# Expert weights in 2 MB chunks with 16 KB rows, and slots chosen by their release

## The chip, the cores and the metric

The kernel runs on one core of a Trainium2 chip. The metric is the time of one execution on the device in microseconds (us), as the median of several runs. The profile shows one execution on the same core.

## The reference

The kernel computes one block of a streaming encoder for 256 tokens of 1024 channels in float32:

```python
ada = c_act @ w_ada + b_ada                      # six vectors of 1024, from the conditioning vector
h = rms_norm(x, norm_mix_g) * (1 + sc_m) + sh_m
x = x + g_m * hybrid_mixer(h)                    # latent attention and a gated convolution, w_in, w_o, ...
h = rms_norm(x, norm_ffn_g) * (1 + sc_f) + sh_f
logits = h @ router_w + router_b                 # 32 experts
top_val, top_idx = top_k(logits, 4); gate_w = softmax(top_val)
# for each expert e, for the tokens that chose it:
gu = h[tok] @ w_gu[e] + b_gu[e]                  # 1024 x 2048
act = (clip(up, -7, 7) + 1) * (g * sigmoid(1.702 * g)),  g = min(gate, 7)
y = act @ w_down[e] + b_down[e]                  # 1024 x 1024
x = x + g_f * sum over the four experts of gate_w * y
return rms_norm(x, norm_final_g)
```

The experts' weights are 32 x (8 MB + 4 MB) = 384 MB; everything else that is loaded is about 52 MB.

## The kernel before

The program has two stages. The front (to about 253 us) computes the conditioning vectors, the mixer and the router. Weights of the front come in 26 units of up to 1 MB (w_in, w_uq, w_ukv, w_up_conv, w_up_attn, w_o); `split` (line 333) turns each raw unit into a high part (ACT, line 336) and a low part (DVE, line 338), and three matmuls (lines 323 to 325, or 448) multiply with them. Between the units stand 16 chunks of w_ada (`ada_next`, line 420). The expert stage goes through 32 experts, each with a capacity of 64 tokens. `gather` (line 958) picks the tokens of four experts by a matmul with one-hot columns; `gate_up` (line 992) makes 64 matmuls with eight 1 MB chunks of w_gu (one chunk: 128 rows of 8 KB, one on each partition); `act` (line 1005) and `act_t` (line 1015, four transposes) follow; `down` (line 1030) makes 16 matmuls with four chunks of w_down (two rows of 4 KB on each partition); `scatter` (line 1044) adds two experts at a time to the result. `down` of an expert runs after `gate_up` of the next one. The last expert's w_down is loaded in columns (line 176, rows of 1 KB), so that the final norm can start on half of them. `beyond` (line 1061) is a branch for experts with more than 64 tokens, in the middle of the experts.

All weights and many intermediate tensors share one ring of 22 slots of 8 KB for each partition (`slot`, line 73): a new tile takes the place of the one that was made 22 tiles earlier, and what is written into it waits until that one was last read. x itself (`xs`) holds a slot too.

The order of work on each engine is the order of the program text (`manual_schedule`). All weight loads are issued by SP. SP goes through its own instructions alone: a load waits there until its slot is free, and all loads behind it wait as well; of the other engines' progress SP sees only what its slots wait for. In the front the order of the loads is written by hand (`queue`, line 361), with tables `LOOK` and `RAW` of how many units ahead are split and loaded. `prefetch(10)` at line 769 puts ten chunks of w_gu ahead of the last w_o units' splits in the text; `bias_load` (line 808, called at 899) loads the experts' bias into a slot of its own, with four loads on SP; `bias_table` (line 816) turns it into a table on ACT and POOL. All further loads of experts stand behind it.

Of the kernel before, what the change touches and what calls it, by code (L numbers as in the profile page):

```python
# [16 lines left out]
P = 128  # L17
D = 1024
# [21 lines left out]
NSLOT = 22  # L40
# [16 lines left out]
def block_kernel(ctx, tc, x, c, positions, w_ada, b_ada, norm_mix_g, w_in, q_norm_g, w_uq, kv_norm_g,  # L57
# [11 lines left out]
    slots = ctx.enter_context(tc.tile_pool(name="slots", bufs=NSLOT))  # L69
# [3 lines left out]
    def slot(shape, name="wslot", dtype=F32):  # L73
        t = slots.tile([P, 2048], dtype, name=name, tag="wslot")
        n = 1
        for s in shape:
            n *= s
        t = t[:, :n]
        if len(shape) == 2:
            t = t.rearrange("p (a b) -> p a b", b=shape[1])  # L80
        elif len(shape) == 3:
            t = t.rearrange("p (a b c) -> p a b c", b=shape[1], c=shape[2])
        return t
# [13 lines left out]
    xs = slot([NT, D], "xs")  # L97
# [10 lines left out]
    iota2 = keep.tile([P, 2, CAP], F32, name="iota2")  # L108
    G.iota(iota2, pattern=[[0, 2], [1, CAP]], base=1, channel_multiplier=0,
# [52 lines left out]
    todo = []  # L162
    for e in range(NE):
        todo += [(e, k) for k in range(NQ)]
        if e and e != NE // 2:
            todo += [(e - 1, k) for k in range(NQ, 12)]
        if e == NE // 2 - 1 or e == NE - 1:
            todo += [(e, k) for k in range(NQ, 12)]
    here = []

    def prefetch(n):
        while len(here) < n and todo:
            e, k = todo.pop(0)
            if e == NE - 1 and k >= NQ:

                w = slot([4, 2, 256])
                b = 4 * ((k - NQ) % 2)
                cols = ap_of(w_down, (e * DE + b * P) * D + 256 * ((k - NQ) // 2),
                             [[D, P], [P * D, 4], [512, 2], [1, 256]])
                for q in ([slice(0, 4)] if k % 2 == 0 else (slice(0, 2), slice(2, 4))):  # L180
                    for h in range(2):
                        load(w[:, q, h], cols[:, q, h])
            elif k < NQ:
                w = slot([2048])
                load(w, gu_v[:, e, k, :])
            else:
                w = slot([2, D])
                load(w, dn_v[:, e, k - NQ])
            here.append(w)

    with tc.tile_pool(name="front", bufs=1) as fr, \
# [13 lines left out]
        pos_i = ft("pos_i", [NT, P], 2, "pe0", I32)  # L205
# [14 lines left out]
        def rows_in(dst, src):  # L220
# [4 lines left out]
                 rows_in(pvec[8:16], norm_ffn_g.rearrange("o (q p) -> (o q) p", p=P)),  # L225
# [24 lines left out]
        def ada0_mm(j):  # L250
            ada_mm(pa, j, ada0[j])

        ss = keep.tile([P, NT], F32, name="ss")
        junk = ft("junk", [P, D], 1, "CT")
# [4 lines left out]
        xn = slot([NT, D], "xn")  # L259
# [31 lines left out]
        for q2 in range(4):  # L291
            p = (mmt() if q2 == 3 else tpt()).rearrange("p (q t) -> p q t", t=T)
            xps.append(p)
            for q in range(2):
                for i in range(NT):
                    TE.transpose(p[:, q, i * P:(i + 1) * P],
                                 xn[:, i, (2 * q2 + q) * P:(2 * q2 + q + 1) * P], ident)
        for j in range(6, 8):
            ada0_mm(j)
        ppc = mmt()  # L300
        TE.transpose(ppc[:, :48], pvec, ident[:48, :48])
        V.tensor_copy(pcol, ppc[:, :48])
        gmix, gffn, qg, kvg = pcol[:, 0:8], pcol[:, 8:16], pcol[:, 16:18], pcol[:, 18:19]
        cw = pcol[:, 19:31].rearrange("p (k q) -> p k q", q=4)

        def halves_t(row, pc):

            for q in range(4):
                TE.transpose(pc[:, q * P:(q + 1) * P], row[:, q * P:(q + 1) * P], ident)
            return pc.rearrange("p (q b r) -> p b q r", b=4, r=32)  # L310
# [4 lines left out]
        arow = ft("arow", [P, 512], 1, "CT")  # L315
        V.tensor_add(arow, brow[0], pa)
        pcv = halves_t(arow, mmt())
# [9 lines left out]
        def cut(pair, *idx):  # L327
            return [t[idx] for t in pair]


        lo_on = "VVVVVVVVVVVVVVVVVVVVVVVVVV"

        def split(raw, shape):
            hi = slot(shape, "whi", F32R)
            lo = slot(shape, "wlo", F32R)
            S.activation(hi, raw, AF.Copy)  # L336
            eng = V if lo_on[len(done)] == "V" else G
            eng.tensor_tensor(lo, raw, hi, op=ALU.subtract)  # L338
            return [hi, lo]
# [18 lines left out]
        raws, done, taken = [], [], [0]  # L358


        queue = list("wwwwwwwawwwwaaaawaawawwawwaaaawwwwwawwwaaw")

        def ada_fetch():
            g, j = ada_todo.pop(0)
            w = slot([2048])
            load(w, ap_of(w_ada, g * 2048 + j * 6 * D, [[8 * 6 * D, P], [1, 2048]]))
            ada_raw.append((g, j, w))

        def fetch(n):
            while len(raws) < min(n, len(jobs)):  # L370
                if queue.pop(0) == "a":
                    ada_fetch()
                else:
                    shape, src = jobs[len(raws)]
                    w = slot(shape)
                    load(w, src)
                    raws.append((w, shape))
# [8 lines left out]
        RAW = [0, 0, 2, 3, 2, 2, 3, 3, 2, 1, 0, 3, 4, 3, 1, 2, 5, 4, 5, 3, 1, 5, 4, 6, 6, 6]  # L386

        def unit():
            k = taken[0]
            taken[0] += 1  # L390
            fetch(k + 1 + LOOK[k] + RAW[k])
            ahead(k + 1 + LOOK[k])
            u = done[k]
            done[k] = None
            return u
# [4 lines left out]
        hT = [slot([NQ, T], "hTh", F32R), slot([NQ, T], "hTl", F32R)]  # L400
        h32 = slot([NQ, T], "h32")
# [11 lines left out]
        S.dma_start(rw, router_w.rearrange("o (q p) e -> p (o q) e", p=P))  # L413
# [3 lines left out]
        ada_todo = [(g, j) for g in (1, 2) for j in range(8)]  # L417
        ada_raw, ada_ps = [], {}

        def ada_next(n=1):  # L420
            for _ in range(n):
                g, j, w = ada_raw.pop(0)
# [21 lines left out]
        def proj(u, ps, half, n):  # L444
            for l, r in ((0, 0), (1, 0), (0, 1)):
                for i in range(NT):
                    for q in range(4):
                        TE.matmul(ps[i][:, :n], hT[l][:, 4 * half + q, i * P:(i + 1) * P], u[r][:, q, :],  # L448
                                  start=(half == 0 and q == 0 and l == 0 and r == 0),
                                  stop=(half == 1 and q == 3 and r == 1), skip_group_check=True)  # L450


        def projT(u, ps, half):
            for m in range(4):
                for q in range(4):
                    mul3(ps[m // 2][:, m % 2, :], cut(u, slice(None), q, slice(m * P, (m + 1) * P)),
                         cut(hT, slice(None), 4 * half + q), half == 0 and q == 0 and m % 2 == 0,
                         half == 1 and q == 3)

# [12 lines left out]
        qq = slot([NT, H, DQK], "qq")  # L472
        kk = slot([NT, H, DQK], "kk")
        vv = slot([NT, H, DV], "vv")
        lat = slot([NT, 384], "lat")
# [19 lines left out]
        CT = ft("CT", [P, 4, T])  # L495
# [53 lines left out]
        cuT = ft("cuT", [P, 4, T + 2])  # L549
        G.memset(cuT[:, :, 0:2], 0.0)  # L550
        for m2 in range(2):
            V.tensor_mul(cuT[:, 2 * m2:2 * m2 + 2, 2:], CT[:, 2 * m2:2 * m2 + 2, :], pu[m2])
# [5 lines left out]
        def qkt(hp):  # L558
            if hp % 2 == 0:
                qkT.append(slot([2, 4, T], "qkT"))  # L560
# [72 lines left out]

        zt = ft("zt", [P, 4, T], tag="CT")

        def conv():
            for m in range(4):
                S.activation(zt[:, m, :], cuT[:, m, 2:], AF.Copy, scale=cw[:, 2, m:m + 1])
            for m in range(4):
                for k in (1, 0):  # L640
                    V.scalar_tensor_tensor(zt[:, m, :], cuT[:, m, k:k + T], cw[:, k, m:m + 1], zt[:, m, :],
                                           op0=ALU.mult, op1=ALU.add)
# [6 lines left out]
        def halves(src, name, engs):  # L649

            t = slot([2, 4, T], name, F32R)
# [4 lines left out]
            return [t[:, 0], t[:, 1]]  # L656
# [3 lines left out]
        def gate(k):  # L660
# [3 lines left out]
            if k % 4 == 0:  # L664
                sg[k // 4] = slot([NT, D], "sg")
# [6 lines left out]
        def branch(src, us, out):  # L672
            ps = [mmt() for _ in range(4)]
            for k in range(2):
                for n in range(4):
# [5 lines left out]
                    if k:  # L681
                        out(i, hs, ps[n])
                yield
# [16 lines left out]
        qkt(3)  # L700
        gate(4)
# [5 lines left out]
        attn = ft("attn", [P, 4, T], tag="cuT")  # L707
# [5 lines left out]
        zT = halves(zt, "zT", (G, V))  # L713
# [3 lines left out]
        pr = scores(3)  # L717
        gate(7)
# [17 lines left out]
        V.tensor_copy(by_half(sh_col[:, 1, :]), halves_t(brow[1], tpt())[:, 2:4, :, 0])  # L736
# [5 lines left out]
        for k in range(4):  # L742
            gate(k)
            if k == 3:
                attnT = halves(attn, "attnT", (G, G))
# [4 lines left out]
        while ada_todo:  # L750
            ada_fetch()
# [11 lines left out]
        while ada_raw:  # L763
            ada_next()
        V.tensor_copy(by_half(a_col[:, 1, :]), halves_t(brow[2], tpt())[:, 0:2, :, 0])
# [13 lines left out]
        def wo_mm(i, h, q0, q1):  # L779
            if q0 == 0:  # L780
                wps[i][h] = mmt()
            for q in range(q0, q1):
                mul3(wps[i][h], cut(mT, slice(None), q, slice(i * P, (i + 1) * P)),
                     cut(wo[q // 2], slice(None), q % 2, slice(h * 512, (h + 1) * 512)), q == 0, q == NQ - 1)

# [8 lines left out]
        def x1_t(i, h):  # L794

            p = tpt().rearrange("p (q t) -> p q t", t=P)
            for q in range(4):
                TE.transpose(p[:, q, :], xs[:, i, (4 * h + q) * P:(4 * h + q + 1) * P], ident)
# [17 lines left out]
        def bias_table():  # L816
# [4 lines left out]
            G.tensor_tensor(bg2[64:], raw[64:], bg2[64:], op=ALU.subtract)  # L821
            for k in range(2):
# [44 lines left out]
        oh0 = ft("oh0", [P, NT, CAP], 1, "cuT")  # L867
# [411 lines left out]
```

## Time and profile before

| | |
|---|---|
| median of 3 runs | 1193.88 us (1189.0 to 1195.42) |
| the profiled execution | 1194.52 us, span 1192.8 us |
| PE busy | 1086.2 us, 91% |
| DVE, ACT, POOL busy | 341.5, 152.6, 29.4 us |
| moved by DMA | 457.70 MB, mean 384 GB/s over the span |
| first load of w_gu | issued at 178.90 us |
| first gate/up matmul | 254.02 us |

The profiled time and the span differ by what lies around the program. A busy PE is not PE at its peak, since matmuls are pipelined and their ends are modelled. The page cuts the span in 40 slices of 29.8 us; the chain of waits is followed back from the last instruction. A DMA in the chain lasts from its issue to its landing, so it includes the transfers ahead of it in the queue. SPq is SP's sequencer, which issues the loads.

### The profile page before, as it was taken

The page shows a single profiled execution, that of the slowest core. Times are in us where ns is not written, and L with a number is a line of the kernel's source. Part 1 is how long each engine was busy: PE and PEld are TensorE (multiplying, and loading weights), DVE is VectorE, ACT ScalarE, POOL GpSimd, SP SyncE. Part 2 cuts the span into 40 slices and gives each one's busy share as a digit, 9 for nine tenths or more (in the row PEclk, how much of TensorE's full clock was granted, in tenths as well). Part 3 has the DMA queues.
Part 4 walks back from the last instruction along what each step waited for, and adds up shares of the span by engine and source line. Part 5 has one row for each costly group of instructions (what it writes and reads, how often), then busy time and mean ns, then how long its engine had stood idle before and what let it go on. Part 6 is the DMA issues. An engine that isn't in the chain of part 4 may idle for free.

```text
span 1192.8 us, 12301 instructions
## 1 busy us (share of the span) xinstructions
PE 1086.2 (91%) x4968; PEld 483.8 (41%) x4968; DVE 341.5 (29%) x694; ACT 152.6 (13%) x261; POOL 29.4 (2%) x86
## 2 busy tenths in 40 slices
PE   5898998989999999999998879999888988898886
PEld 1887666754343343333332243343223322342223
DVE  3857544333221231122212121222112211222113
ACT  1545532212000010000000000010000000000001
POOL 1000001010000000000000000000000000000000
PEclk9898998979999999998999989999999999999999
DMA  9983778589999999999999999999999999999995
GB/s 363 339 330 149 275 309 352 196 347 397 417 417 417 417 416 417 417 417 417 417 417 417 414 419 416 416 417 416 418 417 416 417 417 417 418 417 418 417 415 204
DMA packets 91961, 457.70 MB, mean 384 GB/s; under 512 B 8495, under 2 KB 13648, under 8 KB 56060
## 3 DMA queue, kind: packets, MB, share of 16 engines
q1 hardware_dynamic: 90634, 456.59, 94.6%
q8 instruction: 41, 0.67, 0.2%
q10 hardware_dynamic: 1186, 0.14, 0.1%
q0 software_dynamic: 80, 0.14, 0.0%
q14 instruction: 20, 0.16, 0.0%
HBM read 455.79 MB, written 1.05 MB: 383 GB/s over the span
## 4 chain that ended last, share of the span: by engine, by line
PE 54%; DMA 41%; DVE 2%; ACT 1%; issue 1%; SPq 0%; DVEq 0%; ACTq 0%
DMA wslot<-in_w_gu 22%; PE pg L1001 18%; DMA wslot<-in_w_down 17%; PE pm L1027 10%; PE mm L448 5%; PE pm L969 4%; PE mm L1047 3%; PE mm L323 2%; PE mm L325 2%; PE mm L324 2%; DMA wslot<-in_w_ada 2%; PE pa L247 1%; PE pm L1018 1%; PE pg L1126 1%; DMA wslot<-in_w_in 1%
## 5 line engine op out<-in xcount | busy, mean ns | idle before, releaser
L1001 PE MATMUL pg<-wslot,hsel 128*64 128x512 f32 x2048 | 464.9, 602 | 32.6 <-DMA wslot<-in_w_gu 32.6
L1001 PEld LDWEIGHTS pg<-wslot,hsel 128*64 128x64 f32 x2048 | 139.3, 138 | 342.2 <-issue 245.4
L1027 PE MATMUL pm<-wslot,aT 128*64 128x512 f32 (+1 forms) x1056 | 231.9, 584 | 16.7 <-DMA wslot<-in_w_down 15.1
L1008 DVE TENSOR_SCALAR ga<-pg 128x512 f32<-128x512 f32 x32 | 22.1, 692 | 462.5 <-PE pg L1001 447.2
L1027 PEld LDWEIGHTS pm<-wslot,aT 128*64 128x64 f32 x1056 | 72.3, 137 | 171.7 <-issue 126.1
L1009 ACT ACTIVATE sgm<-ga 128x512 f32<-128x512 f32 x32 | 20.1, 630 | 695.7 <-DVE ga L1008 695.7
L1041 DVE TENSOR_TENSOR yp<-gfx,pm 64x512 f32<-64x512 f32 x62 | 42.5, 685 | 208.3 <-PE pm L1027 207.7
L338 DVE TENSOR_TENSOR wlo<-wslot,whi 128x2048 fp32r<-128x2048 f32 (+3 forms) x26 | 56.2, 2199 | 22.5 <-ACT whi L336 19.8
L969 PE MATMUL pm<-oh,xs 128*128 128x256 f32 (+1 forms) x256 | 58.2, 387 | 4.7 <-DVE oh L955 4.7
L969 PEld LDWEIGHTS pm<-oh,xs 128*128 128x128 f32 x256 | 48.9, 197 | 17.4 <-issue 11.2
L1047 PE MATMUL mm<-yp,s 128*128 128x512 f32 x120 | 54.9, 600 | 0.8 <-DVE yp L1041 0.8
L336 ACT ACTIVATE whi<-wslot 128x2048 fp32r<-128x2048 f32 (+3 forms) x26 | 46.8, 1840 | 17.3 <-DMA wslot<-in_w_in 12.5
L247 PE MATMUL pa<-wslot,cact 128*32 128x512 f32 x192 | 30.2, 718 | 12.3 <-DVE rs_v L116 8.5
L1047 PEld LDWEIGHTS mm<-yp,s 128*128 128x128 f32 x120 | 22.1, 190 | 30.0 <-issue 27.5
L1123 POOL CAST sel<-id 128x256 fp32r<-128x256 f32 x32 | 12.9, 403 | 816.4 <-PE pg L1126 816.4
L1018 PE MATMUL pm<-ident,sgm 128*128 128x128 f32 x128 | 20.9, 286 | 10.4 <-ACT s L989 7.9
L323 PE MATMUL mm<-hTh,whi 128*128 128x256 f32 x96 | 27.5, 287 | 0.0
L325 PE MATMUL mm<-hTh,wlo 128*128 128x256 f32 x96 | 27.2, 283 | 0.0
L324 PE MATMUL mm<-hTl,whi 128*128 128x256 f32 x96 | 27.2, 283 | 0.0
L448 PE MATMUL mm<-whi,hTh 128*128 128x512 f32 (+1 forms) x80 | 23.7, 440 | 3.0 <-ACT hTh L405 3.0
L1126 PE MATMUL pg<-bg,sel 128*128 128x512 f32 x64 | 24.2, 460 | 1.3 <-DVE hsel L156 1.3
L1020 DVE COPY aT<-pm 128x512 f32<-128x512 f32 x32 | 22.1, 691 | 8.3 <-PE pm L1018 6.6
(301 smaller groups left out, 755.2 us busy)
## 6 DMA issues: line engine op xcount, KB each, us to landing
wslot<-in_w_gu SPq DMA_DIRECT2D x256, 1024.0 KB, 20.1
wslot<-in_w_down SPq DMA_DIRECT2D x124, 1024.0 KB, 20.1
wslot<-in_w_ada SPq DMA_DIRECT2D x24, 1024.0 KB, 6.6
wslot<-in_w_in SPq DMA_DIRECT2D x14, 1024.0 KB, 6.5
wslot<-in_w_o SPq DMA_DIRECT2D x4, 1024.0 KB, 8.5
wslot<-in_w_up_conv SPq DMA_DIRECT2D x2, 1024.0 KB
wslot<-in_w_up_attn SPq DMA_DIRECT2D x2, 1024.0 KB, 4.9
wslot<-in_w_down SPq DMA_DIRECT2D x4, 512.0 KB, 8.4
```

Source lines behind the costliest of these rows:

```text
L247: TE.matmul(pa[32 * b:32 * b + 32, :], cact[:, j:j + 1].to_broadcast([P, 32]), w[:, b * 512:(b + 1) * 512], start=(j == 0), stop=(j == 7), ...
L323: TE.matmul(o, l[0], r[0], start=start, stop=False, skip_group_check=True)
L324: TE.matmul(o, l[0], r[1], start=False, stop=False, skip_group_check=True)
L325: TE.matmul(o, l[1], r[0], start=False, stop=stop, skip_group_check=True)
L336: S.activation(hi, raw, AF.Copy)
L338: eng.tensor_tensor(lo, raw, hi, op=ALU.subtract)
L448: TE.matmul(ps[i][:, :n], hT[l][:, 4 * half + q, i * P:(i + 1) * P], u[r][:, q, :], start=(half == 0 and q == 0 and l == 0 and r == 0), st ...
L969: TE.matmul(p[:, q, :], xs[:, i, qs], oh[:, i, :n], start=(i == 0), stop=(i == NT - 1))
L1001: TE.matmul(pg[64 * g:64 * g + 64, n, :], hs[k // 4][:, k % 4, c0:c0 + CAP], w[:, f0:f0 + 512], start=False, stop=(k == NQ - 1), skip_grou ...
L1027: TE.matmul(py[64 * h:64 * h + 64, :], aT[:, qa, 64 * g:64 * g + 64], w[:, h], start=(b == 0), stop=(b == 7), skip_group_check=True)
L1041: V.tensor_mul(yp[64 * k2:64 * k2 + 64, h * 512:(h + 1) * 512], gfx[hp, :], py[hp, :])
L1047: TE.matmul(acc[i][h], s2[:n, i * P:(i + 1) * P], yp[:n, h * 512:(h + 1) * 512], start=start, stop=False, skip_group_check=True)
```

## The change

The ring becomes a list of 22 slots (`Slots`). A tile takes the free slot that was given back longest ago in the order of the program text; once no load is left in the list, one whose neighbour is held comes first, so that neighbours come free together. Tiles are given back by hand (`give`, `drop`). Loads stand in one list (`loads`), and `pump` issues them after each `give` as long as more than `spare` slots are free; `need` issues what is due. x moves out of the slots; the convolution's, the latents' and the attention's tensors move into them.

After the front the 22 slots are joined in pairs to 11 slots of 16 KB (`wide`). Expert weights come in chunks of 2 MB: of w_gu two neighbouring rows (16 KB) lie on a partition, of w_down four neighbouring rows (16 KB). So channel 2(128a + p) + b is on partition p, and the tokens, the norm's columns and the transposes are read with a step of 2 (`fcols`) or 4 (`a[:, q::4]`). `prefetch(10)` is gone; the list of expert loads is filled behind the front's text.

```diff
-NSLOT = 22
+WIDE = 11
-    def slot(shape, name="wslot", dtype=F32):
-        t = slots.tile([P, 2048], dtype, name=name, tag="wslot")
+    class Slots:
+        def __init__(self, pool, since, size):
+            self.pool, self.since, self.held, self.clock, self.spare = pool, since, {}, max(since), 0
+            for i in range(len(since)):
+                pool.tile([P, size], F32, name="w", tag=f"w{i}", bufs=1)
+        def take(self, shape, dtype=F32):
+            i = min((not loads and self.since[(i ^ 1) % len(self.since)] is not None, c, i)
+                    for i, c in enumerate(self.since) if c is not None)[2]
+            self.since[i] = None
+            t = self.pool.tile([P] + list(shape), dtype, name="w", tag=f"w{i}", bufs=1)
+            self.held[id(t)] = (t, i)
+            return t
+        def give(self, *ts):
+            for t in ts:
+                self.clock += 1
+                self.since[self.held.pop(id(t))[1]] = self.clock
+            self.pump()
+        def pump(self):
+            while loads and sum(c is not None for c in self.since) > self.spare:
+                loads.pop(0)()
+    loads = []
+    def need(ready):
+        while not ready():
+            loads.pop(0)()
+    early = ctx.enter_context(ExitStack())
+    narrow = Slots(early.enter_context(tc.tile_pool(name="narrow", bufs=1)), [0] * (2 * WIDE), 2048)
+    slot, give, pump = narrow.take, narrow.give, narrow.pump
...
-    xs = slot([NT, D], "xs")
+    xs = keep.tile([P, NT, D], F32, name="xs")
...
-    gu_v = w_gu.rearrange("o e (q p) f -> p (o e) q f", p=P)
-    dn_v = w_down.rearrange("o e (k q p) d -> p (o e) k q d", q=2, p=P)
+    gu_v = w_gu.rearrange("o e (a p b) f -> p (o e) a b f", p=P, b=2)
+    dn_v = w_down.rearrange("o e (g p q) d -> p (o e) g q d", p=P, q=4)
+    def fcols(k):
+        return slice(256 * (k // 2) + k % 2, 256 * (k // 2) + 256, 2)
...
-                 rows_in(pvec[8:16], norm_ffn_g.rearrange("o (q p) -> (o q) p", p=P)),
+                 rows_in(gvec, norm_ffn_g.rearrange("o (a c) -> (o a) c", c=256)),
...
+        for b in range(2):
+            TE.transpose(ppc[:, 48 + 4 * b:52 + 4 * b], gvec[:, b::2], ident[:4, :4])
...
-        queue = list("wwwwwwwawwwwaaaawaawawwawwaaaawwwwwawwwaaw")
+        loads += [(chunks if c == "a" else units).pop(0) for c in "wwwwwwwwwaaawwawwwwaaaawwwaawaawwwawawaaww"]
+        narrow.spare = 9
         def ahead(n):
-            fetch(n)
             while len(done) < min(n, len(jobs)):
+                need(lambda: len(raws) > len(done))
                 done.append(split(*raws[len(done)]))
...
-        prefetch(10)
         wo = [unit(), unit()]
         next(br)
-        mT = [slot([NQ, T], "mTh", F32R), slot([NQ, T], "mTl", F32R)]
+        give(sg[1])
+        mT = [slot([NQ, T], F32R), slot([NQ, T], F32R)]
         merge_t(0)
         wo += [unit(), unit()]
...
+    early.close()
+    wide = Slots(ctx.enter_context(tc.tile_pool(name="wide", bufs=1, reuse_waits="tile")),
+                 [max(narrow.since[2 * i:2 * i + 2]) for i in range(WIDE)], 4096)
+    slot, give, pump = wide.take, wide.give, wide.pump
...
+    for e in range(NE):
+        loads += [whole([2, 2048], gu_v[:, e, a]) for a in range(4)]
+        for d in ([e - 1] if e and e != NE // 2 else []) + ([e] if e == NE // 2 - 1 else []):
+            loads += [whole([4, D], dn_v[:, d, g]) for g in range(2)]
+    loads += [quarters(NE - 1, c) for c in range(2)]
+    pump()
...
-                    TE.matmul(p[:, q, :], xs[:, i, qs], oh[:, i, :n], start=(i == 0), stop=(i == NT - 1))
+                    TE.matmul(p[:, q, :], xs[:, i, fcols(2 * q2 + q)], oh[:, i, :n], start=(i == 0), stop=(i == NT - 1))
...
         for k in range(NQ):
-            w = chunk(k)
+            if k % 2 == 0:
+                w = chunk(k)
+            gu_block(pg, hs, c0, k, w[:, k % 2, :])
+            if k % 2:
+                give(w)
...
-        sgm = mo.tile([P, 512], F32, name="sgm")
+        sgm = mo.tile([P, 512], F32, name="sgm", bufs=1)
...
-            TE.transpose(p[:, q, :], a[:, q * P:(q + 1) * P], ident)
+            TE.transpose(p[:, q, :], a[:, q::4], ident)
...
-        if e == 0:
+        if e == 7:
+            wide.spare = 1
+        if e == 8:
+            wide.spare = 0
+            bd = slot([3, D])
+            bdn, wT = bd[:NE, 0], bd[:NE, 1, :T]
             G.dma_start(bdn, b_down.rearrange("o e d -> (o e) d"))
+        if e == half - 2:
+            wide.spare = 2
...
-        if e == 18:
+        if e == 27:
+            wide.spare = 1
+        if e == 28:
+            wide.spare = 0
+            fin = slot([3, D])
+            gfin_b, o = fin[:, 0], fin[:, 1:]
```

## Rows read from the trace of the kernel before

**Rows 1.** The page: GB/s of the 40 slices, packets, the chain's shares.
```profile
GB/s 363 339 330 149 275 309 352 196 347 397 417 417 417 417 416 417 417 417 417 417 417 417 414 419 416 416 417 416 418 417 416 417 417 417 418 417 418 417 415 204
DMA packets 91961, 457.70 MB, mean 384 GB/s; under 512 B 8495, under 2 KB 13648, under 8 KB 56060
...
PE 54%; DMA 41%; DVE 2%; ACT 1%; issue 1%; SPq 0%; DVEq 0%; ACTq 0%
```

**Rows 2.** Windows in the expert stage; the last three columns: PEclk, DMA share, GB/s.
```profile
563.00:578.00 15.00, 15.00 (x63) 8.48 (x63) 3.82 (x7) 2.46 (x5) 0.00 (x0) 1.00 1.01 422
...
673.50:688.50 15.00, 13.38 (x54) 4.54 (x56) 4.83 (x7) 0.63 (x1) 0.00 (x0) 1.00 1.03 409
694.50:728.50 34.00, 28.48 (x112) 14.38 (x110) 5.71 (x19) 2.04 (x4) 0.91 (x2) 0.90 1.01 419
```

**Rows 3.** SP's loads from 600 to 735 us; then line 185, issue to landing.
```profile
635.85 17.96 SPq L185 DMA_DIRECT2D wslot<-in_w_gu  x8
655.98 21.77 SPq L188 DMA_DIRECT2D wslot<-in_w_down  x8
677.84 36.70 SPq L185 DMA_DIRECT2D wslot<-in_w_gu  x16
...
DMA to landing us min/median/max: 6.8/20.1/20.7
```

**Rows 4.** The chain in order of time: start, duration, what.
```profile
511.80 20.55 DMA wslot<-in_w_down
...
1138.36 20.34 DMA wslot<-in_w_gu
1158.73 1.94 PE pg L1001 x8
1160.67 3.63 PE mm L1047 x8
...
1168.48 7.39 PE pm L1027 x48
```

**Rows 5.** SP's loads before the experts, and one of SP's waits.
```profile
178.90 19.96 SPq L185 DMA_DIRECT2D wslot<-in_w_gu  x10
214.37 2.47 SPq L813 DMA_DIRECT2D wslot<-in_b_gu  x4
...
237.86 1.96 SPq L188 DMA_DIRECT2D wslot<-in_w_down  x4
244.06 0.34 SPq L185 DMA_DIRECT2D wslot<-in_w_gu  x1
...
SPq L813 <- DVE m L829: 15.5, 1, 15.5
```

**Rows 6.** The last splits: timelines of ACT and DVE around 210 us.
```profile
205.14 1.91 ACT L336 ACTIVATE whi<-wslot 128x2048 fp32r<-128x2048 f32 x1
209.41 1.92 ACT L336 ACTIVATE whi<-wslot 128x2048 fp32r<-128x2048 f32 x1 [2.36 <-DVE wlo L338]
...
204.45 0.69 DVE L690 TENSOR_TENSOR sg<-sg 128x512 f32<-128x512 f32 x1
...
207.08 2.29 DVE L338 TENSOR_TENSOR wlo<-wslot,whi 128x2048 fp32r<-128x2048 f32 x1 [0.74 <-ACT whi L336]
212.05 2.29 DVE L338 TENSOR_TENSOR wlo<-wslot,whi 128x2048 fp32r<-128x2048 f32 x1 [2.68 <-PE tp L757]
```

**Rows 7.** The chain at experts 0, 1, 7, 9; then act_t's weight loads.
```profile
254.02 15.11 PE pg L1001 x64
...
275.45 13.88 PE pg L1001 x64
...
438.40 7.10 PE pm L969 x32
...
485.22 13.88 PE pg L1001 x64
...
1167.82 0.42 PEld L1018 LDWEIGHTS pm<-ident,sgm 128*128 128x128 f32 x4 [0.81 <-issue]
```

More of the change, by code (lines that the diff above doesn't have):

```diff
@@ L251, in ada0_mm @@
             ada_mm(pa, j, ada0[j])
+            give(ada0[j])
         ss = keep.tile([P, NT], F32, name="ss")
-        junk = ft("junk", [P, D], 1, "CT")
+        junk = slot([D])
         for i in range(NT):
@@ L258, in block_kernel @@
         rsqrt_mean(r0, ss, D)
-        xn = slot([NT, D], "xn")
+        give(junk)
+        xn = slot([NT, D])
         V.tensor_scalar(xn[:, 0, :], xs[:, 0, :], r0[:, 0:1], None, op0=ALU.mult)
@@ L327, in cut @@
         def cut(pair, *idx):
-            return [t[idx] for t in pair]
-        lo_on = "VVVVVVVVVVVVVVVVVVVVVVVVVV"
+            return [t[idx] for t in pair[:2]]
         def split(raw, shape):
-            hi = slot(shape, "whi", F32R)
-            lo = slot(shape, "wlo", F32R)
+            hi = slot(shape, F32R)
+            lo = slot(shape, F32R)
             S.activation(hi, raw, AF.Copy)
-            eng = V if lo_on[len(done)] == "V" else G
-            eng.tensor_tensor(lo, raw, hi, op=ALU.subtract)
+            V.tensor_tensor(lo, raw, hi, op=ALU.subtract)
+            give(raw)
             return [hi, lo]
@@ L655, in halves @@
                 engs[m2].tensor_sub(t[:, 1, ms, :], src[:, ms, :], t[:, 0, ms, :])
-            return [t[:, 0], t[:, 1]]
+            give(whole)
+            return [t[:, 0], t[:, 1], t]
         gate_ps = {}
@@ L700, in block_kernel @@
         qkt(3)
+        give(qq, kk)
         gate(4)
@@ L717, in block_kernel @@
         pr = scores(3)
+        give(qkT[1])
         gate(7)
@@ L821, in bias_table @@
             G.tensor_tensor(bg2[64:], raw[64:], bg2[64:], op=ALU.subtract)
+            give(raw)
             for k in range(2):
@@ L910, in block_kernel @@
         wo_mm(1, 1, 6, 8)
+        give(*mT)
         topk(0)
@@ L990, in spread, with gu_block @@
         return s2
+    def gu_block(pg, hs, c0, k, w):
+        for n in range(2):
+            for g in range(2):
+                f0 = n * DE + g * 512
+                TE.matmul(pg[64 * g:64 * g + 64, n, :], hs[k // 4][:, k % 4, c0:c0 + CAP], w[:, f0:f0 + 512],
+                          start=False, stop=(k == NQ - 1), skip_group_check=True)
     def gate_up(hs, c0, bias, chunk):
@@ L996, in gate_up @@
         for k in range(NQ):
[L997 to L1002 removed]
+            if k % 2 == 0:
+                w = chunk(k)
+            gu_block(pg, hs, c0, k, w[:, k % 2, :])
+            if k % 2:
+                give(w)
         return pg
@@ L1028, in down_block, with scaled @@
                       stop=(b == 7), skip_group_check=True)
-    def down(aT, chunk, yp, k2, late=None):
-        py = pmt()
-        for k in range(4):
-            if k == 2 and late is not None:
-                late = act_t(late)
-            w = chunk(k).rearrange("p q (h c) -> p q h c", h=2)
-            for q in range(2):
-                down_block(py, aT, 2 * k + q, w[:, q])
+    def scaled(yp, py, k2):
         for h in range(2):
@@ L1041, in down @@
             V.tensor_mul(yp[64 * k2:64 * k2 + 64, h * 512:(h + 1) * 512], gfx[hp, :], py[hp, :])
+    def down(aT, chunk, yp, k2, late=None):
+        py = pmt()
+        for g in range(2):
+            if g == 1 and late is not None:
+                late = act_t(late)
+            w = chunk(g)
+            v = w.rearrange("p q (h c) -> p q h c", h=2)
+            for q in range(4):
+                down_block(py, aT, 4 * g + q, v[:, q])
+            give(w)
+        scaled(yp, py, k2)
         return late
@@ L1050, in chunk @@
     def chunk(k):
-        prefetch(1)
+        need(lambda: here)
         return here.pop(0)
@@ L1070, in beyond @@
         re = keep.tile([P, 5, NT, 1], F32, name="re")
-        row = slot([2, 2, 512], "row")
-        ring = [slot([2, D], "ring") for _ in range(4)]
+        row = slot([2, 2, 512])
+        ring = slot([2, 2 * D])
         reg = nc.values_load(flag[0:1, 0:1], min_val=0, max_val=T)
@@ L1114, in beyond @@
                 scatter(s2, yp, CAP)
+        give(row, ring)
     acc = [[mmt(), mmt()] for _ in range(NT)]
```

252 lines of the change are left out of this document (124 added, 128 removed).

## The prediction

> **What bounds the kernel now.** I read the page's slices first. From about 300 us on the rate stands at 414 to 419 GB/s in every slice but the last two; in the front it falls to 149 and 196 in two slices [rows 1]. The chain gives PE 54% and DMA 41% [rows 1], so neither share says alone what a faster stream is worth. The chain in order of time does: up to 511.80 it is PE work, then the pieces are DMAs of 20 us, one behind the other, up to the last gate/up chunk [rows 4]. So in the expert stage the end is set by when the stream of expert weights starts and by its pace; PE catches up with a stream that had a lead. Three numbers decide: the start, the time per MB, and what follows the last chunk.
>
> **Pace of the stream.** The loads are 8 MB of w_gu (8 KB rows) and 4 MB of w_down (4 KB rows) for an expert, in that order, with two experts' w_down together at the middle [rows 3]. Stretches in which only 8 KB rows move run at 422 and 419 GB/s (420 weighted by length), the one with 4 KB rows alone at 409, all at a DMA share of 1.01 to 1.03, that is, with all engines busy [rows 2]. For one of 16 engines this is 8192 B / (420/16) = 312.1 ns for an 8 KB row and 160.2 ns for a 4 KB row. Two short rows cost 320.4, one long one 312.1: 8.3 ns are paid per row, whatever its length. An estimate for a 16 KB row on that line is 2 x 312.1 - 8.3 = 615.9 ns (425.6 GB/s). An expert is now 64 rows of each kind an engine, 64 x (312.1 + 160.2) = 30.23 us; after the change 48 x 615.9 = 29.56 us. The difference, 0.67 us over 12 MB, is 0.055 us/MB. The pace as the chain shows it: 8 MB for expert 0 and 12 for each of experts 1 to 10 make the w_down chunk that lands at 511.80 + 20.55 = 532.35 the 128th; the last w_gu chunk, landing at 1138.36 + 20.34 = 1158.70, is the 376th [rows 4]. So 626.35 us / 248 = 2.526 us/MB, and after the change 2.471.
> Bounds for what no row shows, a 16 KB row: if the rows are moved in pieces as now, 2.526 (no gain); if the 8.3 ns vanished altogether, 48 x 607.6 = 29.16 us, or 2.437. I take the line through the two measured sizes.
> The Trainium skill ("DMA: Bandwidth & Descriptors", Why small descriptors are slow) puts the fixed cost at about 3 cycles a packet beside one cycle for 32 bytes: 131, 259 and 515 cycles for 4, 8 and 16 KB. By it the step from 4 to 8 KB would be worth 1.2%; the trace shows 2.8% [rows 2], so the trace does not bear the rule's size out. With the rule's size the pace would be 2.502, near what rival 2 below has by another way.
>
> **Start of the stream.** Now ten w_gu chunks are issued from 178.90 on, ahead of b_gu's four loads at 214.37 [rows 5], because prefetch(10) stands in the text before the last units. In the diff the wide pool is opened behind the whole front: on SP every expert load stands behind bias_load. I followed takes and gives of the narrow list through 26 units and 16 w_ada chunks. The last w_o load waits for the slot of a unit that is split long before, and then SP has only bias_load in front of it. Its slot is the oldest free one whose neighbour is held, the raw slot of the last w_o unit, free when that unit's low part is subtracted (L338). That is also what it waits for now, 15.5 us at L813 [rows 5]: the subtraction runs from 212.05 to 214.34 [rows 6].
> One piece goes: the copy before it (L336) stood still 2.36 us until another subtraction gave up a slot [rows 6]. In the new list its two slots were left by attnT and sg[1], the latter at 204.45 + 0.69 = 205.14. So the copy starts at 207.05, and the subtraction follows the one that ends at 209.37: 209.4 to 211.7. Four issues of b_gu take 2.47 us [rows 5], and the first expert chunk is issued at 214.2, some 35 us later than now.
> Five pairs of slots are free by then (those of hT, of the last w_ada chunks, va, and of w_o's raws): 10 MB, enough until 239. The next five are left by w_o's units and mT, where now w_down's loads start at 237.86, and the eleventh by the bias table, as w_gu now at 244.06 [rows 5]. These 22 MB last until about 271, and expert 0 gives back its first pair when 16 of its 64 matmuls are done, 254.02 + 15.11/4 = 257.8 [rows 7]. I expect no gap.
> An issue lands at the earliest 6.8 us later, as the second of two back to back [rows 3], and the first issue takes 0.34 [rows 5]: 7.2 - 2 x 2.53 = 2.1 to 2.2 us on top of the transfers. So the 376th MB lands at 214.2 + 2.2 + 376 x 2.471 = 1145.5, against 1158.70: 13.2 us earlier. The late start costs 7.5 us (at the present pace it would land at 1166.2), the longer rows bring 20.7.
>
> **What follows the last chunk.** A chunk is now 4 KB x 4 or 8 KB x 2: when the last w_gu chunk lands, 16 matmuls wait for it instead of 8, 1.5 us more than the 1.94 shown; the pieces behind it, up to the 7.39 from 1168.48 on, are PE's, not DMA's [rows 4]. Against that 4 MB of w_down are 0.2 us quicker; the last 4 MB keep their 1 KB rows. Together +1.3.
>
> **Edits at nothing.** gvec: two transposes and a copy near 30 us, on PE and DVE, hidden behind the first unit's split, 0.3 us of front if not; the stream does not start from there. conv, cz, va, lc, junk: the same operations in other slots, or fewer. bdn, dg, wT and gfin_b in slots: their loads stand on POOL's queue, and POOL's next work, sel, is due an expert later; one wide slot less for some experts leaves 10, and what is in flight (20.3 us from issue to landing at 2.53 us a MB [rows 4]) is eight loads. sgm with one buffer: written a whole expert after it was last read.
> Weights are read with a step: act_t's four loads (step 16 bytes) and gather's 32 (8 bytes). They load now in 0.42 us for four, or 105 ns each, under a matmul; gather's 32 matmuls take 7.10 us, 222 ns each [rows 7]. At worst I let a load take four times as long: act_t +1.28 us an expert, gather 32 x (420 - 222) = 6.3 us every fourth expert, 1.6 an expert. PE takes 26.2 us an expert (275.45 to 485.22 for eight) [rows 7], and from 254 to 1145 it has 28.3 for each of 31.5: 2.1 us cover it. I take nothing and keep 2.9 as the other end.
>
> **Sum.** The profiled execution took 1194.52 us with a span of 1192.8, 0.64 above the median shown. 1194.5 - 13.2 + 1.3 = 1182.6; against the median 1182.
>
> **Rivals.**
> 1. The rows are not joined: source and slot are described as two or four rows, and the engines move 8 or 4 KB as now. The late start stays, nothing pays for it: 216.4 + 376 x 2.526 = 1166.2, and 1194.5 + 7.5 + 1.3 = 1203, slower. It decides as soon as the pace stays above (1158.7 - 1.3 - 216.4)/376 = 2.503. For it: no row of a weight load is over 8 KB in this trace. Against: both sides are contiguous over the whole 16 KB, and an 8 KB row moves as one packet now (35,901 packets of 8 KB or more [rows 1], against 256 + 24 loads of w_gu and w_ada with 128 rows each).
> 2. A 16 KB row costs as much as two of 8 KB: only w_down gains, 64 x 160.2 - 32 x 312.1 = 0.27 us an expert, 2.504 us/MB; the 376th lands at 1157.9 and the sum is 1195, no change. The cost a row between 4 and 8 KB speaks against it. The Trainium skill's rule above would give this size too.
> 3. bias_load does not hold SP (another slot is chosen). The stream starts near 183 and fills all 22 MB before expert 0; the next chunk then waits for 257.8, and the 376th lands at 257.8 + 2.2 + 354 x 2.471 = 1134.7: 1172. Against it is the list as I followed it.
> 4. Stepped weight loads make PE the bound: 2.9 us an expert against 2.1 of cover, 0.8 x 32 = 26 us on the PE side, near 1200. It decides from 2.1 us an expert on. The Trainium skill ("SBUF — State Buffer", Specifications) asks for two hits in a 16-byte line; by it the 8-byte step is free and only act_t would pay, which the cover holds. No row here shows a stepped load.
>
> **Chances.** Forecast 0.62 (1173 to 1191), rival 1 0.11, rival 2 0.12, rival 3 0.06, rival 4 0.04, and 0.05 for a stall of SP at a place that I did not see. About 0.5%, or 6 us, is what a measurement can tell here: faster below 1188, slower above 1200. Faster: 0.57 of the forecast and rival 3, 0.63; within: 0.05 of the forecast, rival 2 and half of rival 4 and of the rest, 0.21; slower 0.16. The range 1168 to 1201 leaves out rival 1 and the edges.
>
> **What would show it.** The first w_gu issue near 214, directly behind b_gu; a DMA rate of 422 to 426 in the slices from 300 us on, and some 51,800 packets, since 380 MB of expert weights go from 64,512 rows to 24,320; no slice below 418 there; a DMA-free stretch between 190 and 214; the last w_gu landing near 1145; PE's period unchanged. A rate that stays at 417 makes the prediction wrong through rival 1, one of 419 or 420 through rival 2, an issue before 200 through rival 3, a slice below 415 with PE at 9 through rival 4.

## The result, and the profile after

The kernel after takes 1182.87 us (median of 5 runs, 1181.07 to 1183.95) against 1193.69 before: a ratio of 0.9914, interval 0.9891 to 0.9938, 1% faster. The forecast was 1182. The profiled execution took 1183.78 us with a span of 1182.1.

The page after: the 40 slices and the packets, to be held against [rows 1].

```profile
GB/s 344 369 263 114 332 218 142 295 426 429 427 427 428 427 427 419 427 429 427 427 428 428 426 426 429 427 427 427 426 429 427 428 426 428 429 426 427 428 419 178
DMA packets 48206, 457.66 MB, mean 387 GB/s; under 512 B 4939, under 2 KB 10088, under 8 KB 20756
```

From the ninth slice on the rate is 426 to 429 GB/s, but for two slices at 419 and the last; before it was 414 to 419 from the eleventh on. The two slices ahead of the ninth, 142 and 295, hold the gap before the late start (352 and 196 stood there before). The same in windows of the kernel after (the last three columns are PEclk, DMA share, GB/s); the last three windows are those of [rows 2]:

```profile
190.00:214.00 24.00, 22.39 (x94) 17.71 (x94) 12.83 (x19) 5.78 (x6) 2.70 (x8) 0.87 0.01 3
214.00:300.00 86.00, 82.05 (x395) 47.79 (x396) 30.03 (x90) 16.86 (x32) 4.79 (x8) 0.92 1.00 417
300.00:700.00 400.00, 379.46 (x1638) 142.19 (x1635) 87.16 (x168) 17.63 (x33) 6.02 (x15) 0.99 1.01 427
563.00:578.00 15.00, 15.00 (x64) 9.04 (x60) 4.73 (x8) 2.67 (x5) 0.00 (x0) 1.00 1.01 430
673.50:688.50 15.00, 14.53 (x60) 5.05 (x56) 3.86 (x6) 0.63 (x1) 0.00 (x0) 1.00 1.00 425
694.50:728.50 34.00, 28.35 (x112) 14.48 (x108) 5.71 (x19) 2.04 (x4) 0.40 (x1) 0.90 1.01 426
```

24 us with a DMA share of 0.01, and from 214 to 300 a share of 1.00, all 16 engines busy: the lost start and the better pace stand side by side. Over the 400 us the rate is 427 GB/s, so a 16 KB row takes 16384 / (427/16) = 613.9 ns on an engine.

SP's loads of b_gu and the first of w_gu in the kernel after, and the longest of SP's waits in 180 to 270 us (these answer to [rows 5]):

```profile
212.83 2.48 SPq L837 DMA_DIRECT2D w<-in_b_gu  x4
215.41 20.56 SPq L981 DMA_DIRECT2D w<-in_w_gu  x8
```
```profile
SPq L837 <- DVE m L854: 21.0, 1, 21.0
```

The first w_gu load goes out at 215.41, directly behind b_gu. The wait is put down to a small DVE instruction (a memset at 212.78) behind the subtraction that frees the slot. ACT's two copies (L346) and DVE's two subtractions (L347) of the last w_o units now run without the stop of [rows 6]:

```profile
206.36 3.72 ACT L346 ACTIVATE w<-w 128x2048 fp32r<-128x2048 f32 x2
```
```profile
208.31 4.50 DVE L347 TENSOR_TENSOR w<-w 128x2048 fp32r<-128x2048 f32 x2 [0.74 <-ACT w L346]
```

The chain of waits of the kernel after in order of time, from 1071 us on (these answer to [rows 4]):

```profile
1071.73 5.67 DMA w<-in_norm_final_g
1077.40 0.14 issue
1077.54 3.75 PE pm L1298 x4
...
1109.28 36.77 DMA w<-in_w_gu
1146.05 0.04 issue
1146.09 3.65 PE pg L1054 x16
1149.75 3.63 PE mm L1117 x8
1153.38 3.58 PE pm L1092 x16
1156.96 0.68 PE pm L1083 x4
1157.64 7.06 PE pm L1092 x48
```

The last w_gu chunk lands at 1109.28 + 36.77 = 1146.05, 12.65 us earlier than before. What follows takes 1182.1 - 1146.05 = 36.05 us instead of 1192.8 - 1158.70 = 34.1.

### The profile page after: what moved, and what is told of

It reads as the page before. It is cut to its first block, busy times and chain, and to the rows that moved or that the text cites. A ratio compares the mean times of both kernels' runs of the same rounds, so it can differ in the third digit from the quotient of the medians.

```text
span 1182.1 us, 11908 instructions
## 1 busy us (share of the span) xinstructions
PE 1077.1 (91%) x4970; PEld 492.1 (42%) x4970; DVE 341.5 (29%) x695; ACT 152.1 (13%) x261; POOL 29.3 (2%) x85
## 2 busy tenths in 40 slices
DMA packets 48206, 457.66 MB, mean 387 GB/s; under 512 B 4939, under 2 KB 10088, under 8 KB 20756
## 5 line engine op out<-in xcount | busy, mean ns | idle before, releaser
L1054 PE MATMUL pg<-w,hsel 128*64 128x512 f32 x2048 | 458.3, 601 | 29.8 <-DMA w<-in_w_gu 29.7
L1054 PEld LDWEIGHTS pg<-w,hsel 128*64 128x64 f32 x2048 | 142.6, 138 | 329.8 <-issue 272.9
L1092 PE MATMUL pm<-w,aT 128*64 128x512 f32 (+1 forms) x1056 | 228.0, 582 | 12.0 <-DMA w<-in_w_down 10.4
L1092 PEld LDWEIGHTS pm<-w,aT 128*64 128x64 f32 x1056 | 74.2, 137 | 161.1 <-issue 133.2
L347 DVE TENSOR_TENSOR w<-w 128x2048 fp32r<-128x2048 f32 (+3 forms) x26 | 56.1, 2199 | 20.0 <-ACT w L346 19.9
L460 PE MATMUL mm<-w 128*128 128x512 f32 (+1 forms) x240 | 59.3, 405 | 2.7 <-ACT w L417 2.7
L335 PE MATMUL mm<-w 128*128 128x256 f32 (+1 forms) x160 | 54.5, 341 | 0.5 <-ACT w L783 0.5
L337 PE MATMUL mm<-w 128*128 128x256 f32 (+1 forms) x160 | 53.1, 332 | 0.2 <-DVE w L784 0.2
L460 PEld LDWEIGHTS mm<-w 128*128 128x128 f32 x240 | 47.3, 199 | 14.1 <-ACT w L417 3.8
L336 PE MATMUL mm<-w 128*128 128x256 f32 (+1 forms) x160 | 52.9, 331 | 0.0
L346 ACT ACTIVATE w<-w 128x2048 fp32r<-128x2048 f32 (+3 forms) x26 | 46.3, 1838 | 15.8 <-DMA w<-in_w_in 15.8
L251 PE MATMUL pa<-w,cact 128*32 128x512 f32 x192 | 29.3, 691 | 16.3 <-DVE rs_v L142 8.4
L335 PEld LDWEIGHTS mm<-w 128*128 128x128 f32 x160 | 30.9, 193 | 6.6 <-issue 2.5
L337 PEld LDWEIGHTS mm<-w 128*128 128x128 f32 x160 | 30.8, 192 | 3.9 <-DVE w L784 1.1
```

The costliest lines, as they stand in the source:

```text
L251: TE.matmul(pa[32 * b:32 * b + 32, :], cact[:, j:j + 1].to_broadcast([P, 32]), w[:, b * 512:(b + 1) * 512], start=(j == 0), stop=(j == 7), ...
L335: TE.matmul(o, l[0], r[0], start=start, stop=False, skip_group_check=True)
L336: TE.matmul(o, l[0], r[1], start=False, stop=False, skip_group_check=True)
L337: TE.matmul(o, l[1], r[0], start=False, stop=stop, skip_group_check=True)
L347: V.tensor_tensor(lo, raw, hi, op=ALU.subtract)
L1054: TE.matmul(pg[64 * g:64 * g + 64, n, :], hs[k // 4][:, k % 4, c0:c0 + CAP], w[:, f0:f0 + 512], start=False, stop=(k == NQ - 1), skip_grou ...
```

## Experiments

The theory was the sum of the prediction: the late start costs the time by which it is late, and longer rows win back more. The rivals: rows gain nothing (1, 2), b_gu does not hold SP (3), and, once the first miss was there, that the start does not count in the kernel before.

**1. The kernel after with b_gu's four loads on POOL's queue**, so that nothing stands in front of the expert loads on SP.

```diff
-    load(raw[64 * k:64 * k + 64, t, :], rows[64 * t:64 * t + 64, :])
+    G.dma_start(raw[64 * k:64 * k + 64, t, :], rows[64 * t:64 * t + 64, :])
```

> The changed kernel, with the four b_gu loads issued from POOL's queue instead of SP's; nothing else differs. Theory: in the changed kernel the expert loads stand on SP behind b_gu's slot until 215.4 us, and that late start costs time at the end one for one. Then here the first w_gu load is issued near 183, five chunks land by 217, the next slots come free at 232 (w_o's units), the last w_gu chunk lands at 232.1 + 2.2 + 366 MB x 2.469 = 1138 instead of 1146.05, and the median falls by 8 us to 1175. Rival (the expert stage is held by PE, not by the stream): the first issue moves forward as well, but the time stays at 1183.

Measured: 1172.31 us, ratio to before 0.9826 (0.9805 to 0.9847), 10.6 us faster than the kernel after. SP's loads, SP's longest wait in 180 to 270 us, the chain's last DMA, and DVE's subtractions of this run:

```profile
183.57 50.70 SPq L981 DMA_DIRECT2D w<-in_w_gu  x8
```
```profile
SPq L981 <- PE tp L866: 21.4, 1, 21.4
```
```profile
1099.49 36.35 DMA w<-in_w_gu
```
```profile
206.61 4.49 DVE L347 TENSOR_TENSOR w<-w 128x2048 fp32r<-128x2048 f32 x2 [0.74 <-ACT w L346]
```

The eight w_gu loads spread over 50.70 us: five pairs of slots are free and filled early (the issues run from 183.57 to 208.96), then SP stands 21.4 us for the next pair, until 230.38. From there the stream has no gap: 230.38 + 2.2 + 366 x 2.469 = 1136.2, and the last chunk landed at 1135.84. So b_gu on SP costs the kernel after its first 10 MB, and this version beats both kernels. The expectation, 1175, was 2.7 us too high. Of the 10.2 us between the landings 1.7 are not b_gu's: the same subtractions ran at 206.61 here and at 208.31 in the run above. Why the front differs by that much was not tried.

**2. The kernel after with the rows as they were** (8 KB and 4 KB), the slots, the list and the late start left as in the kernel after. The lines left out put the norm's gain, the router's weights, the last expert's w_down and `beyond` back to the old order.

```diff
-    gu_v = w_gu.rearrange("o e (a p b) f -> p (o e) a b f", p=P, b=2)
-    dn_v = w_down.rearrange("o e (g p q) d -> p (o e) g q d", p=P, q=4)
+    gu_v = w_gu.rearrange("o e (a b p) f -> p (o e) a b f", p=P, b=2)
+    dn_v = w_down.rearrange("o e (g q p) d -> p (o e) g q d", p=P, q=4)
...
-        return slice(256 * (k // 2) + k % 2, 256 * (k // 2) + 256, 2)
+        return slice(k * P, k * P + P)
...
-            TE.transpose(p[:, q, :], a[:, q::4], ident)
+            TE.transpose(p[:, q, :], a[:, q * P:(q + 1) * P], ident)
...
```

> The changed kernel with its slots, its 2 MB loads and its order, but with the old rows: a load of w_gu has two separate rows of 8 KB for each partition, one of w_down four of 4 KB, and the stepped reads of tokens and activations are contiguous again. Theory (the fixed time for each row is what the change saves): the rate falls back to 417 GB/s, 2.526 us/MB, the last w_gu chunk lands 376 x 0.057 = 21 us later, and the median is 1204, slower than before the change by 10. Rival (half as many loads, or other slots, bring the gain): 427 GB/s and 1183. Between them, a part each: 1190 to 1197.

Measured: 1204.38 us, ratio 1.0085 (1.0069 to 1.0101): slower than before. SP's start, the window of 400 us and the last w_gu:

```profile
213.78 20.50 SPq L981 DMA_DIRECT2D w<-in_w_gu  x8
```
```profile
300.00:700.00 400.00, 371.35 (x1600) 137.03 (x1598) 85.70 (x165) 17.62 (x33) 6.02 (x15) 0.98 1.02 416
```
```profile
1138.57 28.35 DMA w<-in_w_gu
```

The rate is back at 416 GB/s. From the first issue to the last landing it is 1166.92 - 213.78 = 953.1 us, after 1146.05 - 215.41 = 930.6: the long rows are worth 22.5 us, and everything else in the change together costs about 11 (8.2 of them by the landing, which was at 1158.70 before).

**3. The kernel before with `prefetch(10)` moved behind the front's text**: the late start alone, as I thought.

```diff
-        prefetch(10)
...
+    prefetch(10)
```

> The kernel before with one call moved: prefetch(10) stands behind the front's text, so that SP issues b_gu's loads ahead of all expert loads, as in the changed kernel. Rows and chunks are the old ones. Theory: the first w_gu load is issued at 217, the 376th MB lands at 217 + 2.2 + 376 x 2.526 = 1169 instead of 1158.7, and the median is 1204; later if the ring's next slots come free later. Rival (the lead of ten chunks is spent waiting for slots anyway): 1194.

Measured: 1190.55 us, ratio 0.9973 (0.9963 to 0.9984). A miss, by 13 us. SP's loads of this run:

```profile
187.31 2.47 SPq L812 DMA_DIRECT2D wslot<-in_b_gu  x4
190.46 42.41 SPq L185 DMA_DIRECT2D wslot<-in_w_gu  x16
235.65 2.65 SPq L188 DMA_DIRECT2D wslot<-in_w_down  x4
241.58 20.41 SPq L185 DMA_DIRECT2D wslot<-in_w_gu  x6
```

The ring goes by the order of the text, so b_gu got another slot, free at 187.31, and the stream began at 190.46, not at 214. But these 11.6 us did not count: the 21st MB was issued at 241.58, in the kernel before at 244.06 [rows 5], and the last w_gu landed at 1155.59 (before 1158.70).

**4. The kernel before with w_down alone in 8 KB rows**: the cost per row by itself.

```diff
-    dn_v = w_down.rearrange("o e (k q p) d -> p (o e) k q d", q=2, p=P)
+    dn_v = w_down.rearrange("o e (k p q) d -> p (o e) k q d", q=2, p=P)
...
-    def act_t(a):
+    def act_t(a, last=False):
...
-            TE.transpose(p[:, q, :], a[:, q * P:(q + 1) * P], ident)
+            c0 = q * P if last else 256 * (q // 2) + q % 2
+            TE.transpose(p[:, q, :], a[:, c0:c0 + P] if last else a[:, c0:256 * (q // 2) + 256:2], ident)
...
-                late = act_t(late)
+                late = act_t(late, True)
...
```

> The kernel before with one kind of row changed: w_down's chunks of 1 MB have two neighbouring rows on a partition (8 KB in one row instead of two of 4 KB), and act_t reads with a step of two elements; the last expert keeps its layout, loads and slots are unchanged. Theory: a row costs 8.3 ns beside its bytes, 32 rows less for each engine and expert save 0.27 us, 31 experts 8.3 us: 1185 to 1186, and the rate in the expert slices rises from 417 to 420 or 421 GB/s. Rival (three cycles of overhead a row, as a rule of a page has it): a third of a per cent, 1190. If stepped weight loads cost PE time that counts, it is above 1190 at the higher rate.

Measured: 1183.49 us, ratio 0.9918 (0.9894 to 0.9941): as expected, a little more. The window of 400 us (417 GB/s in the kernel before) and the last w_gu:

```profile
300.00:700.00 400.00, 384.24 (x1654) 143.01 (x1650) 87.25 (x168) 17.61 (x33) 5.33 (x14) 0.98 1.01 421
```
```profile
1130.46 19.88 DMA wslot<-in_w_gu
```

The landing moves from 1158.70 to 1150.35, 8.35 us. By 8.3 ns a row it is 64 x 160.2 - 32 x 312.1 = 0.27 us an expert, 8.2 us over the 31 whose w_down is loaded in such rows.

**5. The kernel before with the ten early loads held back until b_gu's are issued**, all slots taken where they were.

```diff
+    put, hold = [load], []
...
+        load = put[0]
...
+        put[0] = lambda *a: hold.append(a)
         prefetch(10)
+        put[0] = load
...
+        for a in hold:
+            load(*a)
```

> The kernel before; the ten early w_gu chunks take their slots where they did, so the ring turns as before, but their loads are issued on SP behind b_gu's four. This holds back the stream alone, which the move of the whole call did not. Theory (start and pace set the end): first w_gu issue at 216.9 us instead of 178.9, the 376th MB lands at 216.9 + 2.2 + 376 x 2.526 = 1169 instead of 1158.7, median 1203 to 1204. Rival (the early chunks only wait in full slots until the experts begin, as the move of the call suggests): 1193.

Measured: 1191.5 us, ratio 0.9981 (0.9965 to 0.9996). A miss in the same way: b_gu's loads waited on SP for the same work as in experiment 3 (a sum on PE, 15.0 us in both), so the edit did not keep the slots as they were; b_gu went out early again, and the stream began at 191.75.

```profile
188.60 2.47 SPq L818 DMA_DIRECT2D wslot<-in_b_gu  x4
191.75 23.36 SPq L906 DMA_DIRECT2D wslot<-in_w_gu  x10
...
242.72 0.34 SPq L188 DMA_DIRECT2D wslot<-in_w_gu  x1
```

**6. The kernel before with b_gu on POOL's queue** (the edit of experiment 1).

> The kernel before with b_gu's loads on POOL's queue, the edit that took 10 us from the changed kernel. Theory: here ten chunks are already issued ahead of it, and the load behind it waits for a w_o unit's slot until 220.4 in any case, so nothing moves: 1192 to 1195. Rival (b_gu on SP costs by itself): 1185 or less.

Measured: 1194.21 us, ratio 1.0003 (0.9985 to 1.0022): no change, as expected. SP then waits for other slots: its sixteen w_gu loads spread from 179.11 over 56.20 us, and the 21st MB is issued at 244.29.

**7. Experiment 5 with b_gu in the slot of the last w_o unit**, so that b_gu, and the stream behind it, must wait as in the kernel after.

```diff
-            raw = slot([2, 512])
+            raw = raws[-1][0][:, 0, :].rearrange("p (a b) -> p a b", b=512)
```

> The kernel before; the ten early w_gu loads are issued behind bias_load, and b_gu's four loads go into the slot of the last w_o unit, so that they wait until that unit's low part is subtracted (near 212 to 214 us), and all expert loads behind them too. My theory (the stream that starts after about 200 us can't fill its 22 MB before expert 0 gives slots back, so each us of start is a us of end): b_gu near 214, first w_gu near 216.5, no gap in the stream after it, the 376th MB lands at 216.5 + 2.2 + 376 x 2.526 = 1168.5, against 1158.7: about 1203. Rival (what the two late starts near 191 us showed: the start of the stream doesn't count in the kernel before): 1190 to 1194. If the first w_gu goes out before 200 us, the run says nothing on this.

Measured: 1202.52 us, ratio 1.0091 (1.0066 to 1.0116). Here the late start costs time. SP's loads, two windows, and the last w_gu:

```profile
208.90 2.47 SPq L818 DMA_DIRECT2D wslot<-in_b_gu  x4
211.48 7.85 SPq L906 DMA_DIRECT2D wslot<-in_w_gu  x10
...
248.17 4.57 SPq L188 DMA_DIRECT2D wslot<-in_w_gu  x1
```
```profile
190.00:214.00 24.00, 23.25 (x106) 18.32 (x105) 12.38 (x16) 5.78 (x6) 2.35 (x8) 0.98 0.11 34
214.00:300.00 86.00, 81.91 (x391) 46.08 (x391) 29.64 (x88) 16.83 (x32) 5.57 (x9) 0.90 1.02 417
```
```profile
1144.20 19.83 DMA wslot<-in_w_gu
```

No gap behind the start, and the sum of the prediction holds: 211.48 + 2.2 + 376 x 2.526 = 1163.5, landed at 1164.03. Of the 9.4 us between the medians 5.3 are this landing and 1.0 a longer tail (1199.1 - 1164.03 = 35.07 us). The other 3 lie in the spread of the executions: the profiled one, at 1200.74 us, is the shortest of its six and 1.8 under their median, and that of the kernel before, at 1194.52, is 1.4 above the 1193.15 of this comparison. That the median came out at the 1203 of the expectation is luck in part: the 1203 was for a start at 216.5, and by the same sum a start at 211.48 gives about 1198.

## Why the prediction was right

**The start.** Predicted 214.2, measured 215.41. The slot, the wait and the stop that goes (2.36 us) were as followed by hand; the subtractions ended at 212.81 instead of 211.7, because the front as a whole came 1.2 us later.

**The price of the start.** Right in size for the kernel after: predicted 7.5 us, and experiment 2, which has the late start and the old rows, landed its last w_gu 8.2 us after the kernel before. Experiment 7 shows 5.3 us of landing for a start 3.9 us earlier than after's. What fell is the theory I drew from it in experiments 3 and 5, that each us of start is one of end in any kernel. They show its limit. The lead cannot exceed the slots: SP had issued 21 MB when it first stood for a slot that expert 0 had to give back, 12.7 us in the kernel before and 12.8 in experiments 3 and 5. These are the issues behind that wait, in this order, then the last w_gu of experiments 3 and 5, and a window of the kernel before and the same of experiment 7 (columns as above):

```profile
257.15 10.63 SPq L185 DMA_DIRECT2D wslot<-in_w_gu  x7
```
```profile
254.79 10.63 SPq L185 DMA_DIRECT2D wslot<-in_w_gu  x7
```
```profile
255.91 10.63 SPq L188 DMA_DIRECT2D wslot<-in_w_gu  x7
```
```profile
1135.75 19.84 DMA wslot<-in_w_gu
```
```profile
1137.11 19.87 DMA wslot<-in_w_gu
```
```profile
252.00:260.00 8.00, 7.17 (x26) 2.45 (x28) 1.88 (x9) 0.00 (x0) 1.54 (x3) 0.72 0.49 167
```
```profile
252.00:260.00 8.00, 8.00 (x38) 2.63 (x36) 0.00 (x0) 0.00 (x0) 0.00 (x0) 0.98 1.01 405
```

So the DMA engines stood still for half of these 8 us in the kernel before (share 0.49; 0.56 and 0.57 in experiments 3 and 5), and not in experiment 7 (1.01). From the issue behind the wait the sum goes on with 376 - 21 = 355 MB: 257.15 + 2.2 + 355 x 2.526 = 1156.1, and 1153.7 and 1154.8; the last w_gu landed 2.6, 1.9 and 2.2 us after that, which was not followed further. In these kernels the end follows the start of expert 0 (see the table), not that of the stream. At 2.526 us a MB, 21 MB take 21 x 2.526 + 2.2 = 55.2 us, so only a start after about 200 us counts (an estimate from these rows). A start at 190.46 or 191.75 is inside, one at 211.48 or 215.41 outside:

| | first w_gu | 21st MB issued | first gate/up matmul | last w_gu landed | median |
|---|---|---|---|---|---|
| before | 178.90 | 244.06 | 253.9 | 1158.70 | 1193.2 to 1193.7 |
| experiment 3 | 190.46 | 241.58 | 251.1 | 1155.59 | 1190.55 |
| experiment 5 | 191.75 | 242.72 | 252.3 | 1156.98 | 1191.5 |
| experiment 6 | 179.11 | 244.29 | 254.2 | 1158.71 | 1194.21 |
| experiment 7 | 211.48 | 248.17 | 247.8 | 1164.03 | 1202.52 |

Before, the early start was mostly given away: SP stood 15.5 us at b_gu [rows 5] and then waited for slots.

**The pace.** Predicted 2.471 us a MB; measured (1146.05 - 215.41 - 2.2) / 376 = 2.469. The line through the two row sizes gave 615.9 ns for 16 KB (425.6 GB/s), the window 613.9 (427). Experiment 4 gives 421 GB/s for 8 KB rows, 311.3 ns, so joining two of them saves 2 x 311.3 - 613.9 = 8.7 ns against 8.3 predicted: about the same price per row between 4 and 8 KB as between 8 and 16. The rates are read to 1 GB/s, which is 1.4 ns of the 613.9, so the price is good to some 2 ns. By it still longer rows have at most 8.7 of 613.9 ns, 1.4%, left to win (an estimate). The Trainium skill ("DMA: Bandwidth & Descriptors", Why small descriptors are slow) has a fixed cost of about 3 cycles a packet, which is the direction seen here; by that size the second step would be worth 0.6%, an estimate from the page. From 421 to 427 it is 1.4%, so the size is not borne out. (The prediction gives the first step as 2.8%; 320.4 over 312.1 is 2.7%.) The Trainium skill ("Perfetto Trace Analysis", Roofline) also calls about 120% of 358 GB/s the practical ceiling of a single core; 427 is 119%, so this trace agrees.

**The landing.** Predicted 1145.5, measured 1146.05; the 0.55 is the start's 1.2 less the pace's 376 x 0.002 = 0.75, to 0.1: two small misses that cancel in part.

**The tail.** Predicted +1.3, measured +1.95. The 16 matmuls took 3.65 instead of 1.94 (+1.7, predicted +1.5), the four transposes 0.68 instead of 0.59, the 48 matmuls 7.06 instead of 7.39: +1.47 together. The other 0.48 is spread over the small pieces behind them. The sum was 1182.6 for the profiled execution, which took 1183.78; the 1.2 are 0.55 of the landing and 0.65 of the tail.

**Edits at nothing.** Stepped loads, held at 0 with 2.9 us an expert as the other end, cost PE time but none that counts. The views are of the transposes' weight loads (the kernel after, step of 16 bytes; before, no step; experiment 4, step of 8 bytes except for the last expert), then of gather's (after, step of 8 bytes; before, no step). Durations in ns are min/median/max:

```profile
L1083 PEld LDWEIGHTS pm<-ident,sgm x128: 195/210/222, 271.6 to 1157.2; 128*128 128x128 f32 x128
```
```profile
L1018 PEld LDWEIGHTS pm<-ident,sgm x128: 137/141/143, 274.3 to 1168.1; 128*128 128x128 f32 x128
```
```profile
L1019 PEld LDWEIGHTS pm<-ident,sgm x128: 138/209/223, 274.7 to 1159.7; 128*128 128x128 f32 x128
```
```profile
L1026 PEld LDWEIGHTS pm<-oh,xs x256: 192/196/336, 266.4 to 1038.2; 128*128 128x128 f32 x128
```
```profile
L969 PEld LDWEIGHTS pm<-oh,xs x256: 186/190/337, 269.1 to 1046.2; 128*128 128x128 f32 x128
```

A stepped load of a transpose takes 69 ns more, half as much again, and one of gather 6 ns more: 4 x 69 ns and, every fourth expert, 32 x 6 ns make 0.3 us an expert, against the 2.1 us of cover in the prediction. The transposes themselves take 284 ns instead of 273. The base of the prediction was low: a load took 141 ns before in act_t and 190 in gather, not 105. The Trainium skill ("SBUF — State Buffer", Specifications) asks for two hits in a 16-byte line, and by it, as the prediction has it, a step of 8 bytes would be free. For act_t the trace does not agree: with a step of 8 bytes (experiment 4) a load took 209 ns, with one of 16 bytes 210. One edit at nothing did show: the norm's gain, whose load now stands on POOL's queue late in the expert stage, was waited for. It is issued at 1071.73, lands 5.67 us later, and PE's transposes (L1298) start behind it. It costs nothing at the end: the slices from 1064 to 1123 us stay at 427 and 428 GB/s, and the last w_gu load, issued at 1109.28, still lands 36.77 us later, behind the loads ahead of it.

**The packets.** Predicted 51,800, measured 48,206. The difference is among the packets under 512 B, 4939 against 8495 [rows 1]: 3556 fewer, which I had left as they were. They go with the number of loads and with the router's weights: experiment 2, with the old rows and as few loads as the kernel after, has 3048 packets fewer than the kernel before on the queue of SP's loads, 16 for each of the 190 loads that are gone; another 512 are on the queue of the router's weights (674 instead of 1186), whose rows are joined as well.

**The rivals.** Rival 1 (rows not joined) was priced at 1203; experiment 2 is that case and took 1204.38. Rival 2 (16 KB as two of 8 KB) falls with the 427 GB/s. Rival 3 (bias_load does not hold SP) was priced at 1172; experiment 1 is that case and took 1172.31. Its working had 22 MB filled early, where only 10 were, and came out right because the next slot came free at 230, not at 257.8. Rival 4 falls with the 0.3 us an expert of the stepped loads.

## What to carry to other kernels

In a stage bound by a stream of loads the end is its start plus its bytes times its pace, but the start counts only from the point where the buffers can no longer be filled before the first of them is given back: work out that point first. Look at what stands in front of the stream on its queue; here four small loads that waited for a slot cost more than 8 us, and moving them to another queue gave that back, while the same move in the kernel before gave nothing. Between 4 and 16 KB longer rows were worth about the same for each row saved (here some 8 to 9 ns on each of 16 engines), so the rates of two row sizes in one trace predicted the third.

## What the runs showed that I had not expected

A start of the weight stream 11.6 us later (experiment 3) came with a kernel that is 0.3% faster, not slower. Its expert 0 begins 2.8 us earlier (first gate/up matmul at 251.1 instead of 253.9) and its last w_gu lands 3.1 us earlier; what makes its front shorter was not tried. And the front moves by 1.6 us between profiled executions of kernels whose fronts hardly differ: b_gu went out at 212.83 in the kernel after and at 211.21 in experiment 2, where only the layout of a few operands of the front is another; so a predicted start is good to about that much.
